# Gathering raw tokens with 1/rms in the one-hot rows, finishing the output projection by token tile, and bias casts on ScalarE, in a one-core hybrid decoder layer

## The chip, the cores and the metric

One NeuronCore of a Trainium2 chip runs the whole layer; the other seven stay idle. The core has five engines with a queue each, worked off in order: PE (TensorE, matrix products), DVE (VectorE), ACT (ScalarE), POOL (GpSimd) and SP (SyncE, which here only issues DMAs). The metric is the device time of one launch in microseconds (us): the median of three runs before is 1156.03 us (1154.72 to 1156.2).

## The reference, cut to what matters

256 tokens of width 1024 go through one layer: two attention branches, their merge and output projection, then an expert network and a gated embedding. The change touches the end of the output projection and the entrance to the experts:

```python
x = x + merged @ w_out                        # residual stream, 256 x 1024
h = rmsnorm(x, g_ffn)                         # x / rms(x) * g_ffn
logits = h @ w_router + b_router              # 32 experts
top_vals, top_idx = lax.top_k(logits, 4)
top_w = softmax(top_vals)                     # each token goes to 4 experts
gu = xb @ w_gate_up[e] + b_gate_up[e]         # xb: the rows of h that chose expert e
g, u = min(gu[:, :1024], 7), clip(gu[:, 1024:], -7, 7)
y = ((u + 1) * g * sigmoid(1.702 * g)) @ w_down[e] + b_down[e]
x = x + (sum over a token's experts of top_w * y)
```

All weights are float32; the 32 experts have 8.4 MB (gate and up) and 4.2 MB (down) each.

## The kernel before, in words

Tokens lie in two tiles (`tt` = 0, 1) of 128 partitions. The residual stream `xs` is a tile of 128 x 2 x 1024 float32. The stages run one after the other: projections, attention with the gate units beside it, the branch merge into `mT`, the output projection (L676 to L696), norm and routing (L700 to L742), and a loop over 32 experts (L991 on).

**The weight stream.** Ten SBUF slots of 2 MB hold what the experts need. `release` (L152) is called where a slot's last user has been written down; it gives the slot to the next 2 MB piece of a fixed sequence (`seq`) and issues its DMA on SP's queue, which then waits until the last user is done. The sequence starts with the four gate/up pieces of expert 0 and the four of expert 1, then the two down pieces of expert 0. Slots 0 and 1 hold operands of the output projection (`mT` in slot 0, split weights in slot 1) and are released at its end (`release(0, 1, 2)`); slot 2 holds split weights of earlier units and is free sooner; slot 3 holds `b96`, the raw gate/up bias, and is released after the bias casts. The eleventh piece of the stream can only be issued when expert 0 has used its first one.

**The output projection.** Its weights come in eight units, each split into a high and a low part (cast on ACT, difference on DVE, L216 and L220). For each half `dh` of the columns and each of four units, twelve matmuls run: six for tile 0, six for tile 1 (three products per piece, L260 to L262). Then DVE adds each tile to `xs` (L694) and ACT takes the sum of squares (L695).

**Routing.** `raw_T(tt, dh)` (L667) transposes half a tile of `xs` on PE (`hT`), copies it on ACT (L672) and multiplies it with the router weights (`lg`, L674). The halves `dh` = 0 of both tiles are done inside the last projection half, the halves `dh` = 1 after it. One `rsqrt` for both tiles (thirteen small DVE operations) gives 1/rms, with which ACT makes `h_perm`, a scaled and permuted copy of `xs` (L717). DVE then picks the top four per token, and PE computes each token's place in its expert's list (`pos`, L739 to L741). `keep_warm` puts idle matmuls into PE's queue, 30 ahead of `pos` and 8 behind it.

**Bias.** `b_gate_up` is held in bfloat16 as three terms: sixteen casts and eight subtractions of 512 columns (L703 to L709), all on DVE.

**Gather.** For each pair of experts DVE builds one-hot rows `oh` from the places, and PE multiplies `h_perm` by them (L814 to L822): 16 matmuls per tile pair and column half. `ow`, the same rows times the router weights (L834), later brings the results back.

A scheduler orders each engine's instructions from the program's order, its dependences and its own cost estimates, so the order that is run differs from that of the code.

Of the kernel before, what the change touches and what calls it, by code (L numbers as in the profile page):

```python
# [65 lines left out]
def hybrid_layer(ctx, tc, x, p, b_down, w_ple_gate, w_ple_proj, bgu3, xt, tabs, wpre, wgu, wdn, out):  # L66
# [15 lines left out]
    def tok(tt):  # L82
        return slice(tt * P, (tt + 1) * P)

    def rsqrt(pool, ss, n, dim, name):

        m = pool.tile([P, n], F32, tag=f"rs_m{n}", name=f"{name}_m")
        V.tensor_scalar(m, ss, 1.0 / dim, EPS, op0=ALU.mult, op1=ALU.add)
        sh = pool.tile([P, n], I32, tag=f"rs_s{n}", name=f"{name}_s")
        V.tensor_single_scalar(sh, m.bitcast(I32), 1, op=ALU.logical_shift_right)  # L90
        r = pool.tile([P, n], F32, tag=f"rs_r{name}", name=f"{name}_r")
        V.tensor_scalar(r.bitcast(I32), sh, -1.0, RSQRT_MAGIC, op0=ALU.mult, op1=ALU.add)
        t = pool.tile([P, n], F32, tag=f"rs_t{n}", name=f"{name}_t")
        for _ in range(3):
            V.tensor_tensor(t, r, r, op=ALU.mult)
            V.scalar_tensor_tensor(t, in0=t, scalar=-0.5, in1=m, op0=ALU.mult, op1=ALU.mult)
            V.scalar_tensor_tensor(r, in0=t, scalar=1.5, in1=r, op0=ALU.add, op1=ALU.mult)
        return r
# [576 lines left out]

    lgb = [bank("lg") for _ in range(2)]  # L676
    for dh in range(2):
        bs = [bank("wo") for _ in range(2)]
        for kk in range(4):
            wh, wl = unit(2)  # L680
            for tt in range(2):
                for j in range(2):
                    k = 2 * kk + j
                    three([(bs[tt], (mT[0][:, k, tok(tt)], mT[1][:, k, tok(tt)]), (wh[:, j], wl[:, j]))],
                          k == 0, k == 7)
            for after, i in ((1, 8), (3, 9)):
                if 4 * dh + kk == after:
                    release(i)
            if dh == 1 and kk == 1:
                raw_T(0, 0)  # L690
                raw_T(1, 0)
        for tt in range(2):
            xv = xs[:, tt, dh * 512:(dh + 1) * 512]
            V.scalar_tensor_tensor(xv, in0=bs[tt], scalar=0.5, in1=xv, op0=ALU.mult, op1=ALU.add)  # L694
            A.activation(bank("sq"), xv, AF.Square, accum_out=hss[:, dh, tt:tt + 1])  # L695
    release(0, 1, 2)  # L696

    for i in range(3):
        r = slice(i * NE, (i + 1) * NE)
        V.tensor_copy(id96[r], ident[r, r])  # L700
    for c in range(0, 2048, 512):
        c = slice(c, c + 512)
        V.tensor_copy(bgu[:, c], b96[:, c])  # L703
        V.tensor_tensor(b96[:, c], b96[:, c], bgu[:, c], op=ALU.subtract)
        V.tensor_copy(bgu[NE:2 * NE, c], b96[NE:2 * NE, c])
        r = slice(2 * NE, 3 * NE)
        V.tensor_copy(bgu[r, c], b96[r, c])
        V.tensor_tensor(b96[r, c], b96[r, c], bgu[r, c], op=ALU.subtract)
        V.tensor_copy(bgu[r, c], b96[r, c])  # L709
    release(3)  # L710
    h_perm = keep.tile([P, 2, D], F32, tag="h8", name="h_perm")
    for tt in range(2):
# [3 lines left out]
    for tt in range(2):  # L716
# [11 lines left out]
    ohe = keep.tile([P, 2, 4, NE], F32, name="ohe")  # L728
    for tt in range(2):
        V.scalar_tensor_tensor(lg[:, tt], in0=lgb[tt][:, :NE], scalar=hrs[:, tt:tt + 1], in1=brb,  # L730
                               op0=ALU.mult, op1=ALU.add)
# [62 lines left out]

    def gather(pm, base):

        oh = work("oh", [P, 2, CAP])
        for tt in range(2):
            V.tensor_scalar(oh[:, tt], iota[:, 0:CAP], float(base), pm(tt), op0=ALU.add, op1=ALU.is_equal)
        b = shared("g")  # L800
        for k in range(8):
            for tt in range(2):
                T.matmul(b[:, k * CAP:(k + 1) * CAP], h_perm[:, tt, k * P:(k + 1) * P], oh[:, tt],
                         start=(tt == 0), stop=(tt == 1))
# [3 lines left out]
        return xg, oh  # L808

    def gather_pair(e):  # L810

        oh = work("oh", [P, 2, 2 * CAP])
        for tt in range(2):
            V.tensor_tensor(oh[:, tt].rearrange("p (j c) -> p j c", j=2), iota.rearrange("p (j c) -> p j c", j=2),  # L814
                            posm[:, tt, e:e + 2].unsqueeze(2).broadcast_to([P, 2, CAP]), op=ALU.is_equal)
        xg = work("xg", [P, 8, 2 * CAP])
        for half in range(2):
            b = psum("gu"[half])
            ks = slice(half * 4, half * 4 + 4)
            for k in range(4):  # L820
# [5 lines left out]
        return xg, oh  # L826

    def weigh(ow, oh, wv_, odd):  # L830
        for tt in range(2):
            o = ow[:, tt].rearrange("p (g c) -> p g c", g=4)
            o = o[:, 1:3] if odd else o[:, 0:4:3]
            V.tensor_scalar(o, oh[:, tt:tt + 1].broadcast_to([P, 2, CAP]), wv_(tt), None, op0=ALU.mult)  # L834

    def weigh_pair(e, oh):
        ow = work("ow", [P, 2, S])
        for j in range(2):
            weigh(ow, oh[:, :, j * CAP:(j + 1) * CAP], wv_of(e + j), j)
        return ow  # L840
# [81 lines left out]
    def overflow(room):  # L922
# [18 lines left out]
        with tc.If(v > OVER):  # L941
            V.memset(ow, 0.0)
            with tc.For_i(0, NE, 1) as e:
# [42 lines left out]

    xg2, oh2 = gather_pair(0)
    weights()
    ow = weigh_pair(0, oh2)
    ht = None  # L990
    for e in range(NE):  # L991
# [166 lines left out]
```

## Time and profile before

| | |
|---|---|
| median of 3 runs | 1156.03 us |
| the profiled execution's own time | 1153.93 us |
| its span, first to last instruction | 1151.9 us |
| PE busy | 1077.9 us (94%) |
| DVE busy | 328.4 us (29%) |
| ACT busy | 209.5 us (18%) |
| POOL busy | 79.0 us (7%) |
| HBM read | 438.21 MB |

The 2.0 us between span and time lie outside the first and last instruction. Times in rows are counted from the span's start. In a timeline row the columns are start, duration, engine, line, operation, what is written and read, shape, and in brackets how long the engine had been idle and whom it waited for. [...]

### The profile page before, as it was taken

What the parts mean: (1) busy time and instruction counts of PE and PEld (TensorE: products, weight loads), DVE (VectorE), ACT (ScalarE), POOL (GpSimd) and SP (SyncE); (2) the same over time, 40 slices, a digit from 0 to 9 for tenths busy, and PEclk for the clock granted to TensorE, in tenths of its full rate; (3) what the DMA queues carried; (4) which work ended last, traced back from release to release, by engine and by line L of the source; (5) the groups of instructions that cost most, each with busy time, mean ns of one, the idle gap of its engine ahead of it and who ended that gap; (6) DMA issues with size and microseconds to landing.
All of it is one profiled execution on the core that took longest, in us unless ns stands there. A gap on an engine that the chain in (4) does not pass through costs nothing. (4 is left out here: it accounts for less than half of the span.)

```text
span 1151.9 us, 13101 instructions
## 1 busy us (share of the span) xinstructions
PE 1077.9 (94%) x5446; PEld 524.7 (46%) x5446; DVE 328.4 (29%) x730; ACT 209.5 (18%) x393; POOL 79.0 (7%) x82
## 2 busy tenths in 40 slices
PE   9799999999999999998889999998998989898988
PEld 7688997543434343342333434343433333333336
DVE  5679688321111121111110111120111111111136
ACT  5576753110000000000001000000000000000024
POOL 5752320000000000000000000000000000000000
PEclk9999999999999999999999999998999999999999
DMA  9544569999999999999999999999999999999991
GB/s 369 189 146 147 183 201 356 374 428 431 432 429 432 430 430 431 431 428 414 430 431 431 429 432 430 430 431 427 431 431 432 427 431 431 430 431 431 428 387 42
DMA packets 40079, 440.15 MB, mean 382 GB/s; under 512 B 4432, under 2 KB 5200, under 8 KB 14832
## 3 DMA queue, kind: packets, MB, share of 16 engines
q1 hardware_dynamic: 40016, 439.27, 91.3%
q8 instruction: 44, 0.72, 0.2%
q14 instruction: 19, 0.16, 0.0%
HBM read 438.21 MB, written 1.05 MB: 381 GB/s over the span
## 5 line engine op out<-in xcount | busy, mean ns | idle before, releaser
L861 PE MATMUL g<-w_g,xg 128*64 128x512 f32 x1024 | 294.5, 600 | 22.0 <-DMA w_g<-in_wgu 17.4
L861 PE MATMUL u<-w_g,xg 128*64 128x512 f32 x1024 | 290.9, 595 | 0.0
L885 PE MATMUL y<-w_d,ht 128*64 128x512 f32 x992 | 227.0, 597 | 11.9 <-DMA w_d<-in_wdn 11.9
L861 PEld LDWEIGHTS g<-w_g,xg 128*64 128x64 f32 x1024 | 78.7, 137 | 167.2 <-issue 122.6
L865 DVE TENSOR_SCALAR g<-g 128x512 f32<-128x512 f32 x32 | 22.1, 692 | 462.2 <-PE g L855 462.2
L861 PEld LDWEIGHTS u<-w_g,xg 128*64 128x64 f32 x1024 | 82.5, 138 | 146.7 <-issue 143.9
L885 PEld LDWEIGHTS y<-w_d,ht 128*64 128x64 f32 x992 | 69.1, 136 | 132.3 <-issue 114.7
L867 ACT ACTIVATE th<-g 128x512 f32<-128x512 f32 x32 | 20.2, 632 | 478.7 <-DVE g L865 478.7
L890 DVE COPY ys<-y 64x512 f32<-64x512 f32 x31 | 21.5, 694 | 168.7 <-ACT ys L889 168.7
L895 PE MATMUL acc<-ys,owT 128*128 128x512 f32 x128 | 59.4, 605 | 8.8 <-ACT ys L889 8.8
L889 ACT COPY ys<-y 64x512 f32<-64x512 f32 x31 | 18.0, 580 | 263.2 <-PE y L885 263.2
L895 PEld LDWEIGHTS acc<-ys,owT 128*128 128x128 f32 x128 | 22.9, 189 | 45.3 <-ACT ys L889 21.1
L822 PE MATMUL g<-oh,h_perm 128*128 128x128 f32 x256 | 33.3, 282 | 6.3 <-DVE g L865 6.2
L822 PEld LDWEIGHTS g<-oh,h_perm 128*128 128x128 f32 x256 | 29.9, 191 | 16.9 <-DVE g L865 11.7
L822 PEld LDWEIGHTS u<-oh,h_perm 128*128 128x128 f32 x256 | 29.8, 192 | 8.1 <-issue 8.1
L220 POOL TENSOR_TENSOR fr<-raw_x,fr 128x384 fp32r<-128x384 f32 (+1 forms) x21 | 29.2, 1399 | 47.8 <-ACT fr L216 47.8
L822 PE MATMUL u<-oh,h_perm 128*128 128x128 f32 x256 | 32.2, 279 | 0.0
L261 PE MATMUL proj<-fr,fr 128*128 128x512 f32 (+1 forms) x64 | 26.2, 409 | 5.6 <-DVE fr L220 5.4
L260 PE MATMUL gate<-fr,fr 128*128 128x256 f32 x104 | 30.5, 293 | 0.0
L262 PE MATMUL gate<-fr,fr 128*128 128x256 f32 x104 | 29.6, 285 | 0.7 <-DVE fr L220 0.7
L834 DVE TENSOR_SCALAR ow<-oh,whalf 128x128 f32<-128x128 f32 x64 | 14.0, 283 | 54.6 <-PE owT L847 54.6
L261 PE MATMUL gate<-fr,fr 128*128 128x256 f32 x104 | 29.4, 283 | 0.0
(320 smaller groups left out, 1161.2 us busy)
## 6 DMA issues: line engine op xcount, KB each, us to landing
w_g<-in_wgu SPq DMA_DIRECT2D x124, 2048.0 KB, 31.9
w_d<-in_wdn SPq DMA_DIRECT2D x62, 2048.0 KB, 32.6
raw_x<-in_wpre SPq DMA_DIRECT2D x29, 512.0 KB, 3.7
w_g<-in_wgu SPq DMA_DIRECT2D x8, 1024.0 KB, 27.9
raw<-in_wpre SPq DMA_DIRECT2D x12, 512.0 KB, 8.3
w_ple<-in_w_ple_gate SPq DMA_DIRECT2D x8, 512.0 KB, 10.0
raw_o<-in_wpre SPq DMA_DIRECT2D x4, 512.0 KB, 5.0
w_d<-in_wdn SPq DMA_DIRECT2D x2, 1024.0 KB, 25.8
```

The source lines that it names most:

```text
L220: o = e.tensor_tensor(lo[:, a:b], src[:, a:b], hi[:, a:b], op=ALU.subtract)
L260: T.matmul(o, lh, rh, start=first, stop=False)
L261: T.matmul(o, lh, rl, start=False, stop=False)
L262: T.matmul(o, ll, rh, start=False, stop=last)
L822: T.matmul(b[:, k * P:(k + 1) * P], h_perm[:, tt, (half * 4 + k) * P:(half * 4 + k + 1) * P], oh[:, tt], start=(tt == 0), stop=(tt == 1))
L861: T.matmul(gu[i][half * CAP:(half + 1) * CAP], xg[:, k], wv_, start=(k == 0), stop=False)
L865: V.tensor_scalar_min(g, gu[0], 7.0)
L867: A.activation(th, g, AF.Tanh, scale=0.851)
L885: T.matmul(y[g * CAP:(g + 1) * CAP], ht[:, f % 4, (f // 4) * CAP:(f // 4 + 1) * CAP], w[:, dh * 512:(dh + 1) * 512], start=(f == 0), stop= ...
L889: A.copy(ys[0:CAP, odd], y[0:CAP])
L890: V.tensor_copy(ys[CAP:P, 1 - odd], y[CAP:P])
L895: T.matmul(acc[tt][dh], owT[:, dh, tok(tt)], ys[:, dh], start=first, stop=last)
```

## The change

Three things are rewritten.

1. In the second half of the output projection, unit 6 isn't used when it comes; units 6 and 7 are used together, first all twelve matmuls of tile 0, then all twelve of tile 1. Residual, second transpose, 1/rms and routing are then written per tile, so that those of tile 0 stand ahead of tile 1's. `tc.issue_after` keeps tile 1's residual behind tile 0's `rsqrt`.
2. `h_perm` is dropped. The gather multiplies `xs` itself, read with a step of 8 elements (`xk`), and 1/rms goes into the one-hot rows (is_equal, then times `hrs`). Since `oh` then holds 1/rms, `ow` is built from the places directly.
3. The sixteen bias casts move from DVE to ACT; the eight subtractions stay on DVE. They are written behind the projection as before.

```diff
-    for tt in range(2):
-        raw_T(tt, 1)
-    V.tensor_tensor(hss[:, 0], hss[:, 0], hss[:, 1], op=ALU.add)
-    hrs = rsqrt(wk, hss[:, 0], 2, D, "f")
-    for tt in range(2):
-        A.activation(h_perm[:, tt].rearrange("p (k q) -> p k q", k=8),
-                     xs[:, tt].rearrange("p (q k) -> p k q", k=8), AF.Copy, scale=hrs[:, tt:tt + 1])
-    keep_warm(WARM2)
...
+    def residual(tt, dh, b):
+        xv = xs[:, tt, dh * 512:(dh + 1) * 512]
+        V.scalar_tensor_tensor(xv, in0=b, scalar=0.5, in1=xv, op0=ALU.mult, op1=ALU.add)
+        A.activation(bank("sq"), xv, AF.Square, accum_out=hss[:, tt, dh:dh + 1])
+
+    hrs = [None, None]
+    for dh in range(2):
+        bs = [bank("wo") for _ in range(2)]
+        late_units = []
+        for kk in range(4):
+            late_units.append((kk, *unit(2)))
+            for after, i in ((1, 8), (3, 9)):
+                if 4 * dh + kk == after:
+                    release(i)
+            if dh and kk == 2:
+                continue
+            for tt in range(2):
+                for k2, wh, wl in late_units:
+                    for j in range(2):
+                        k = 2 * k2 + j
+                        three([(bs[tt], (mT[0][:, k, tok(tt)], mT[1][:, k, tok(tt)]), (wh[:, j], wl[:, j]))],
+                              k == 0, k == 7)
+                if dh and kk == 3:
+                    with tc.issue_after(last_step[0]) if tt else ExitStack():
+                        residual(tt, 1, bs[tt])
+                    raw_T(tt, 1)
+                    V.tensor_tensor(hss[:, tt, 0:1], hss[:, tt, 0:1], hss[:, tt, 1:2], op=ALU.add)
+                    hrs[tt] = rsqrt(keep, hss[:, tt, 0:1], 1, D, f"f{tt}")
+                    route(tt)
+            late_units = []
+            if dh == 1 and kk == 1:
+                raw_T(0, 0)
+                raw_T(1, 0)
+        if not dh:
+            for tt in range(2):
+                residual(tt, 0, bs[tt])
+    release(0, 1, 2)
...
-        V.tensor_copy(bgu[:, c], b96[:, c])
+        A.copy(bgu[:, c], b96[:, c])
         V.tensor_tensor(b96[:, c], b96[:, c], bgu[:, c], op=ALU.subtract)
-        V.tensor_copy(bgu[NE:2 * NE, c], b96[NE:2 * NE, c])
+        A.copy(bgu[NE:2 * NE, c], b96[NE:2 * NE, c])
         r = slice(2 * NE, 3 * NE)
-        V.tensor_copy(bgu[r, c], b96[r, c])
+        A.copy(bgu[r, c], b96[r, c])
         V.tensor_tensor(b96[r, c], b96[r, c], bgu[r, c], op=ALU.subtract)
-        V.tensor_copy(bgu[r, c], b96[r, c])
+        A.copy(bgu[r, c], b96[r, c])
...
+    xk = [xs[:, tt].rearrange("p (q k) -> p k q", k=8) for tt in range(2)]
...
         for tt in range(2):
-            V.tensor_tensor(oh[:, tt].rearrange("p (j c) -> p j c", j=2), iota.rearrange("p (j c) -> p j c", j=2),
-                            posm[:, tt, e:e + 2].unsqueeze(2).broadcast_to([P, 2, CAP]), op=ALU.is_equal)
+            for j in range(2):
+                V.tensor_scalar(oh[:, tt, j * CAP:(j + 1) * CAP], iota[:, 0:CAP], posm[:, tt, e + j:e + j + 1], hrs[tt],
+                                op0=ALU.is_equal, op1=ALU.mult)
...
-                    T.matmul(b[:, k * P:(k + 1) * P], h_perm[:, tt, (half * 4 + k) * P:(half * 4 + k + 1) * P],
+                    T.matmul(b[:, k * P:(k + 1) * P], xk[tt][:, half * 4 + k],
                              oh[:, tt], start=(tt == 0), stop=(tt == 1))
```

**ACT's queue** at the end of the output projection, before: `fr_80<-raw_x` and `fr_80<-pre_64` are the casts of units 6 and 7, `sq,fss<-xs` the squares, `raw_x<-hT` the copies of the transposes.

```order
L216 CAST fr_80<-raw_x 128x1024
L216 CAST fr_80<-pre_64 128x1024
L695 ACTIVATE sq,fss<-xs 128x512 x2
L672 COPY raw_x<-hT 128x4x128 x2
L695 ACTIVATE sq,fss<-xs 128x512 x2
L672 COPY raw_x<-hT 128x4x128 x2
L717 ACTIVATE h_perm<-xs,f_r 128x1024 x2
```

The same place in ACT's queue now, where `bgu<-b_1928` are the bias casts:

```order
L742 CAST bgu<-b_1928 96x512 x4
L218 CAST fr_80<-raw_x 128x1024
L744 CAST bgu<-b_1928 32x512
...
L702 ACTIVATE sq,fss<-xs 128x512
L218 CAST fr_80<-pre_64 128x1024
L702 ACTIVATE sq,fss<-xs 128x512
L748 CAST bgu<-b_1928 32x512
...
L746 CAST bgu<-b_1928 32x512
L748 CAST bgu<-b_1928 32x512
L674 COPY raw_x<-hT 128x4x128 x2
L702 ACTIVATE sq,fss<-xs 128x512
```

All sixteen casts now stand ahead of the first copy `raw_x<-hT`: four, then three, then nine directly in front of it.

**PE's queue** at the end of the output projection, before (`wo` the projection, `hT` the transposes, `lg` the router logits):

```order
L261 MATMUL wo<-fr_80,fr_79 128x512
L262 MATMUL wo<-fr_80,fr_79 128x512
L671 MATMUL hT<-cst,xs 128x128 x8
L281 LDWEIGHTS warm
L281 MATMUL warm<-warm 128x256
...
L674 MATMUL lg<-cst,raw_x 128x32 x4
L281 LDWEIGHTS warm
L281 MATMUL warm<-warm 128x256
L674 MATMUL lg<-cst,raw_x 128x32 x4
```

And now, from eight projection matmuls before the end:

```order
L673 MATMUL hT<-cst,xs 128x128 x4
L263 MATMUL wo<-fr_80,fr_79 128x512
L264 MATMUL wo<-fr_80,fr_79 128x512
...
L263 MATMUL wo<-fr_80,fr_79 128x512
L676 MATMUL lg<-cst,raw_x 128x32 x4
L264 MATMUL wo<-fr_80,fr_79 128x512
...
L264 MATMUL wo<-fr_80,fr_79 128x512
L673 MATMUL hT<-cst,xs 128x128 x4
L283 LDWEIGHTS warm
L283 MATMUL warm<-warm 128x256
```

Tile 0's second transposes and logits have moved in front of the last eight and four projection matmuls. The first halves, earlier on, keep their places: four `wo`, then `lg` for tile 0, `hT` for tile 1, four `wo`, `lg` for tile 1. SP's queue has the same order in both.

## Rows read from the trace of the kernel before

**Rows 1.** Windows: busy us by engine, granted clock, DMA share, GB/s.

```profile
300.00:600.00 300.00, 284.74 (x1380) 111.65 (x1376) 49.94 (x96) 20.93 (x37) 0.00 (x0) 1.00 1.01 429
198.00:200.00 2.00, 1.58 (x11) 1.10 (x11) 0.86 (x3) 1.44 (x5) 0.00 (x0) 1.00 0.94 344
212.00:220.00 8.00, 8.00 (x39) 2.66 (x39) 1.09 (x3) 0.00 (x0) 0.00 (x0) 1.00 0.65 229
```

**Rows 2.** Timeline of SP's queue: weight pieces issued around the routing.

```profile
189.04 0.33 SPq L80 DMA_DIRECT2D w_d<-in_wdn  x1
197.29 0.80 SPq L80 DMA_DIRECT2D w_g<-in_wgu  x2
215.93 10.63 SPq L80 DMA_DIRECT2D w_g<-in_wgu  x4
```

**Rows 3.** Timeline of PE: end of the output projection.

```profile
190.22 1.06 PE L674 MATMUL lg<-cst,raw_x 128*128 128x32 f32 x8
194.13 0.39 PE L262 MATMUL wo<-fr,fr 128*128 128x512 f32 x1
196.87 0.39 PE L262 MATMUL wo<-fr,fr 128*128 128x512 f32 x1
```

**Rows 4.** Timeline of DVE and ACT: first bias cast, first copy, `h_perm`.

```profile
180.22 0.42 DVE L703 CAST bgu<-b 96x512 bf16<-96x512 f32 x1 [2.08 <-DMA b<-in_bgu]
189.56 0.59 ACT L672 COPY raw_x<-hT 128x512 f32<-128x512 f32 x1 [2.76 <-PE hT L671]
202.50 4.19 ACT L717 ACTIVATE h_perm<-xs,f_r 128x1024 f32<-128x1024 f32 x2 [1.65 <-DVE f_r L97]
```

**Rows 5.** Windows: the stretch between the first bias cast and the first copy.

```profile
180.22:189.56 9.34, 9.34 (x45) 7.75 (x44) 9.16 (x15) 3.45 (x6) 0.00 (x0) 1.00 1.01 428
```

**Rows 6.** Timeline of ACT: two casts back to back.

```profile
46.86 1.03 ACT L216 CAST fr<-raw_x 128x1024 fp32r<-128x1024 f32 x1
47.79 1.04 ACT L216 CAST fr<-raw 128x1024 fp32r<-128x1024 f32 x1
```

**Rows 7.** Groups by shape, ACT and DVE, 512 columns: count | busy, mean ns | idle.

```profile
L216 ACT CAST fr<-raw_x 128x512 fp32r<-128x512 f32 x1 | 0.6, 623 | 0.3 <-PE proj L262 0.3
...
L708 DVE TENSOR_TENSOR b<-b,bgu 32x512 f32<-32x512 f32 x4 | 2.7, 684 | 0.1
```

**Rows 8.** Timeline of PE: restarts after two long waits.

```profile
44.43 0.50 PE L261 MATMUL proj<-fr,fr 128*128 128x512 f32 x1 [2.78 <-DVE fr L220]
57.33 0.50 PE L261 MATMUL proj<-fr,fr 128*128 128x512 f32 x1 [2.66 <-DVE fr L220]
```

**Rows 9.** Windows: the clock behind the first of these restarts.

```profile
44.00:46.00 2.00, 1.57 (x5) 1.33 (x6) 1.25 (x7) 0.54 (x2) 0.00 (x0) 0.80 0.21 37
46.00:48.00 2.00, 2.00 (x6) 1.51 (x6) 0.08 (x1) 2.00 (x5) 0.04 (x1) 0.50 0.61 225
48.00:50.00 2.00, 2.00 (x15) 1.83 (x14) 1.88 (x2) 1.97 (x4) 2.00 (x2) 0.85 0.18 29
```

**Rows 10.** Timeline of DVE and PE: selection done, places begun.

```profile
204.14 0.66 DVE L737 TENSOR_REDUCE sel<-ohe 128x32 f32<-128x128 f32 x2
206.76 0.31 PE L739 MATMUL pos<-sel,cst 128*128 128x32 f32 x2
```

**Rows 11.** One tile's or line's loads: count, ns min/median/max, first and last start.

```profile
L822 PEld LDWEIGHTS g<-oh,h_perm x256: 186/192/192, 208.5 to 1042.3; 128*128 128x128 f32 x128
L671 PEld LDWEIGHTS hT<-cst,xs x16: 138/140/226, 188.6 to 199.1; 128*128 128x128 f32 x16
L1042 PEld LDWEIGHTS y<-cst,xs x4: 189/192/193, 1122.6 to 1122.9; 128*128 128x128 f32 x4
```

**Rows 12.** Timeline of PE: bias matmuls of two experts, two experts apart.

```profile
402.37 0.40 PE L855 MATMUL g<-bgu,id 96*64 96x512 bf16 x2
455.65 0.40 PE L855 MATMUL g<-bgu,id 96*64 96x512 bf16 x2
```

More of the change, by code (lines that the diff above doesn't have):

```diff
@@ L83, in tok @@
         return slice(tt * P, (tt + 1) * P)
+    last_step = [None]
     def rsqrt(pool, ss, n, dim, name):
@@ L96, in rsqrt @@
             V.scalar_tensor_tensor(t, in0=t, scalar=-0.5, in1=m, op0=ALU.mult, op1=ALU.mult)
-            V.scalar_tensor_tensor(r, in0=t, scalar=1.5, in1=r, op0=ALU.add, op1=ALU.mult)
+            last_step[0] = V.scalar_tensor_tensor(r, in0=t, scalar=1.5, in1=r, op0=ALU.add, op1=ALU.mult).ins
         return r
@@ L674, in raw_T @@
             T.matmul(lgb[tt][:, :NE], hrT[:, k, tok(tt)], w_r[:, k], start=(k == 0), stop=(k == 7))
[L676 to L680, printed above, removed]
-            for tt in range(2):
[L682 to L691, printed above, removed]
-        for tt in range(2):
[L693 to L702, printed above, removed]
-        V.tensor_copy(bgu[:, c], b96[:, c])
-        V.tensor_tensor(b96[:, c], b96[:, c], bgu[:, c], op=ALU.subtract)
-        V.tensor_copy(bgu[NE:2 * NE, c], b96[NE:2 * NE, c])
-        r = slice(2 * NE, 3 * NE)
-        V.tensor_copy(bgu[r, c], b96[r, c])
-        V.tensor_tensor(b96[r, c], b96[r, c], bgu[r, c], op=ALU.subtract)
-        V.tensor_copy(bgu[r, c], b96[r, c])
-    release(3)
-    h_perm = keep.tile([P, 2, D], F32, tag="h8", name="h_perm")
-    for tt in range(2):
-        raw_T(tt, 1)
-    V.tensor_tensor(hss[:, 0], hss[:, 0], hss[:, 1], op=ALU.add)
-    hrs = rsqrt(wk, hss[:, 0], 2, D, "f")
-    for tt in range(2):
-        A.activation(h_perm[:, tt].rearrange("p (k q) -> p k q", k=8),
-                     xs[:, tt].rearrange("p (q k) -> p k q", k=8), AF.Copy, scale=hrs[:, tt:tt + 1])
-    keep_warm(WARM2)
     sel = keep.tile([P, 2, NE], F32, name="sel")
@@ L728, in hybrid_layer, with route @@
     ohe = keep.tile([P, 2, 4, NE], F32, name="ohe")
-    for tt in range(2):
-        V.scalar_tensor_tensor(lg[:, tt], in0=lgb[tt][:, :NE], scalar=hrs[:, tt:tt + 1], in1=brb,
+    lgb = [bank("lg") for _ in range(2)]
+    def route(tt):
+        V.scalar_tensor_tensor(lg[:, tt], in0=lgb[tt][:, :NE], scalar=hrs[tt], in1=brb,
                                op0=ALU.mult, op1=ALU.add)
@@ L737, in hybrid_layer @@
         V.tensor_reduce(sel[:, tt], ohe[:, tt].rearrange("p j e -> p e j"), axis=AX.X, op=ALU.add)
+    def residual(tt, dh, b):
[34 more added lines that the diff above has]
+    release(0, 1, 2)
+    for i in range(3):
+        r = slice(i * NE, (i + 1) * NE)
+        V.tensor_copy(id96[r], ident[r, r])
+    for c in range(0, 2048, 512):
+        c = slice(c, c + 512)
+        A.copy(bgu[:, c], b96[:, c])
+        V.tensor_tensor(b96[:, c], b96[:, c], bgu[:, c], op=ALU.subtract)
+        A.copy(bgu[NE:2 * NE, c], b96[NE:2 * NE, c])
+        r = slice(2 * NE, 3 * NE)
+        A.copy(bgu[r, c], b96[r, c])
+        V.tensor_tensor(b96[r, c], b96[r, c], bgu[r, c], op=ALU.subtract)
+        A.copy(bgu[r, c], b96[r, c])
+    release(3)
+    keep_warm(WARM2)
     b = bank("pos")
@@ L793, in down_bias, with gather @@
                 T.matmul(acc[tt][dh], wT[:, tok(tt)], bdn[:, dh * 512:(dh + 1) * 512], start=False, stop=False)
-    def gather(pm, base):
+    xk = [xs[:, tt].rearrange("p (q k) -> p k q", k=8) for tt in range(2)]
+    def gather(pm):
         oh = work("oh", [P, 2, CAP])
         for tt in range(2):
-            V.tensor_scalar(oh[:, tt], iota[:, 0:CAP], float(base), pm(tt), op0=ALU.add, op1=ALU.is_equal)
+            V.tensor_scalar(oh[:, tt], iota[:, 0:CAP], pm(tt), hrs[tt], op0=ALU.is_equal, op1=ALU.mult)
         b = shared("g")
@@ L802, in gather @@
             for tt in range(2):
-                T.matmul(b[:, k * CAP:(k + 1) * CAP], h_perm[:, tt, k * P:(k + 1) * P], oh[:, tt],
+                T.matmul(b[:, k * CAP:(k + 1) * CAP], xk[tt][:, k], oh[:, tt],
                          start=(tt == 0), stop=(tt == 1))
@@ L825, in gather_pair, with weigh @@
                             gpk[:, 1, ks].unsqueeze(2).broadcast_to([P, 4, 2 * CAP]), op=ALU.mult)
-        return xg, oh
-    def weigh(ow, oh, wv_, odd):
+        return xg
+    def weigh(ow, pm, wv_, odd):
         for tt in range(2):
@@ L949, in overflow @@
                 for c in EXTRA_CHUNKS:
-                    xg, oh = gather(lambda tt: pmd[:, tt:tt + 1], c * CAP)
-                    weigh(ow, oh, lambda tt: wvd[:, tt:tt + 1], 0)
+                    V.tensor_scalar_add(pmd, pmd, float(-CAP))
+                    xg = gather(lambda tt: pmd[:, tt:tt + 1])
+                    weigh(ow, lambda tt: pmd[:, tt:tt + 1], lambda tt: wvd[:, tt:tt + 1], 0)
                     owT = combine_T(ow)
@@ L1005, in hybrid_layer @@
         if odd and not last:
-            xg2, oh2 = gather_pair(e + 1)
-            ow = weigh_pair(e + 1, oh2)
+            xg2 = gather_pair(e + 1)
+            ow = weigh_pair(e + 1)
         ht = hidden_T(u, "th" if last else "ht")
```

12 lines of the change are left out of this document (6 added, 6 removed).

## The prediction

> **What bounds the kernel now.** I read the windows first. From 300 to 600 us the DMA engines are busy all the time and move 429 GB/s [rows 1]. A 2 MB piece (2.10 MB) thus takes 4.9 us, and the 12.6 MB of one expert 29.3 us. PE, busy as it looks, does two experts in 53.3 us [rows 12], against 58.7 us for their weights; it starts the experts behind the stream, since ten slots are full by then, and catches up. So the end of the program is the end of the weight stream, and a microsecond in which the stream stands still while its slots are blocked is a microsecond of time. What PE, DVE or ACT do is worth something only where it moves such a standstill.
>
> The windows show where the stream stands still around the change: from 198 to 200 the rate is 344 GB/s, 0.4 us lost; from 212 to 220 it is 229 GB/s, (429 - 229) x 8 / 429 = 3.7 us lost [rows 1]. SP's queue says why [rows 2]. The first down piece is issued at 189.04. The next pieces wait for slots 0 and 1, which the last projection matmul frees (it starts at 196.87 and ends at 197.26 [rows 3]), and are issued at 197.29, just before the queue runs dry at about 198.5. With the piece behind them they last 3 x 4.9 = 14.7 us, to about 213.7 (a window that loses 0.4 lies between). The next issue is at 215.93, when expert 0 has used its first piece: 2.2 us too late, and 3.7 - 2.2 = 1.5 us more until the stream is back at full rate. Both places together cost 4.1 us, and that is the most this change can win.
>
> So two distances count: when the projection ends, and how long it is from there to expert 0's first release (215.93 - 197.26 = 18.7 us now).
>
> **Bias casts on ACT.** The bias arrives at 180.22 [rows 4]. From there to the first copy `raw_x<-hT` at 189.56, ACT is busy 3.45 us of 9.34 [rows 5]. All sixteen casts now stand ahead of that copy. ACT's cast of 512 columns takes 0.62 us [rows 7], and of back-to-back casts the second starts 0.1 us before the first one's end (47.79 against 46.86 + 1.03 [rows 6]), so 0.52 us each: 8.3 us. ACT then has 3.45 + 8.3 = 11.8 us of work from 180.22, to 192.0. The last of the four chunks is a chain of cast, subtraction on DVE (0.68 us [rows 7]) and cast, with nothing to fill it: 192.7. The copy ends 0.6 us later, at 193.3. PE has four projection matmuls and then, in its queue, the logits of this very copy; before, it began them at 190.22 [rows 3], now at 193.4. Everything behind them on PE waits, the rest of the projection first: **3.1 us**. Bounds, since no row shows an ACT cast to bfloat16: with DVE's 0.42 us [rows 4] for each and no wait in the last chain, the logits start at 191.3 (a stall of 1.1 us); with the full 0.62 us, no overlap and the wait, at 195.0 (4.8 us). I take the value of the ACT row. The time that DVE is relieved of (its casts) is worth nothing: it would have ended before 197.26 in any case.
>
> **Projection by token tile.** Tile 0's transposes and logits have moved ahead of the last eight and four projection matmuls. Their price on PE comes from what they take now: from 190.22 to 194.13 PE does two sets of logits, one of transposes and seven projection matmuls; twelve such matmuls take 196.87 - 194.13 = 2.74 us, seven 1.6 us, so 2.3 us remain, and one set of each costs about 1.35 us. The projection therefore ends at 197.26 + 3.1 + 1.35 = 201.7.
>
> **The clock.** A stall of 3.1 us is long for PE. After waits of 2.78 and 2.66 us [rows 8] PE restarts at full clock, and behind the first of them the granted clock is 0.80, 0.50 and 0.85 in the next six microseconds [rows 9]: (0.20 + 0.50 + 0.15) x 2 = 1.7 us lost. Here the stretch behind the stall is solid projection, so I add 1.7 us: the projection ends at **203.4**. Bounds: 0 and 1.7.
>
> **From there to the first release.** Before, the selection of both tiles is done at 204.80, but the places wait on PE to 206.76, behind idle matmuls [rows 10]: 2.0 us. `h_perm` (4.19 us from 202.50 [rows 4]) ends before that and costs nothing, so neither does dropping it win anything on this path. With tile 0's routing off the path (it runs beside tile 1's matmuls) I take away another 1.1 us, the second residual, square and copy; two more small DVE operations for the one-hot rows give 0.2 back. That is 18.7 - 2.0 - 1.1 + 0.2 = 15.8 us; bounds 14.5 (the idle matmuls never in the way) and 18.7 (all stays).
>
> **The sum.** With the projection's end at 203.4 the two pieces are issued 4.9 us after the queue ran dry at 198.5 (its piece of 189.04 hangs on unit 5, which the change leaves where it is); with the 1.5 us of a restart 6.4 us are lost. The three pieces then last to 203.4 + 1.5 + 14.7 = 219.6, and expert 0's first release comes at 203.4 + 15.8 = 219.2. An issue 1.2 us ahead of running dry lost 0.4 us, one at that point would lose 1.5, so 0.4 ahead costs about 1.1. Together 7.5 us instead of 4.1: **3.4 us slower**. The profiled execution took 1153.93 us (span 1151.9), so it would take 1157.3; that execution is 2.1 us below the median of 1156.03, so the median becomes **1159.4 us**.
>
> **The gather.** A pair's 16 gather matmuls now load `xs` with a step of 32 bytes. The trace has this step: transposes of such columns load in 192 ns against 140 ns for contiguous ones, while the gather's loads take 192 ns already [rows 11]. If they grew by the same 52 ns and all of it showed, the 32 loads in the trace would cost 1.7 us a pair. PE's spare time of 58.7 - 53.3 = 5.4 us a pair covers that in the loop; only the first gather, ahead of the first release, would pay it. I take 0 for the loop and for the first gather, and keep 1.7 as the other end. [...] The DVE operations per pair (four instead of two for `oh`) lie in PE's spare time too.
>
> **Rivals.**
> - *The clock holds.* Same stall, projection end at 201.7: 3.2 + 1.5 = 4.7 us, and the second place as above 1.1: 1.7 us slower, 1157.7. For it: the part behind the stall begins with logits and transposes, not with the same work as in rows 8. Against: both waits of that length were followed by the low clock.
> - *ACT's casts are no bottleneck* and the change does what its parts suggest. The copy isn't late; the projection ends at 197.26 + 1.35 = 198.6, the issue comes as the queue runs dry (1.5 us lost), the pieces last to 214.8, the release comes at 214.4 (1.1 us lost): 2.6 instead of 4.1, so 1.5 us faster, 1154.5. With the shortest distance, 14.5, the second loss is about 0.2: 2.4 us faster, 1153.6. It decides from the point where ACT's work ahead of the copy fits into the 5.9 us that were idle, 0.37 us a cast; no row of ACT with 512 columns is that short.
> - *The strided read shows.* 1.7 us more on the first gather: the release comes 1.3 us after running dry instead of before it, 2.8 us lost there instead of 1.1: 1161.1 with the stall and the low clock. For it: rows 11. Against: a load lies beside the matmul ahead of it.
>
> **Chances and range.** My forecast 0.46, the clock holds 0.25, ACT no bottleneck (or a stall near its lower bound) 0.20, strided read 0.09. Two kernels within 0.2%, 2.3 us, can't be told from no change here: below 1153.7 is faster, above 1158.3 slower. Slower takes 0.37 of my forecast (the rest of it, with a milder loss, is within), 0.03 of the second case and all of the last: 0.49. Faster needs the best form of the third case: 0.13. The same: 0.38. The range goes from 1153.7, at the better end of the third case, to 1161.8, above the last.
>
> **What would show it.** In the changed profile ACT's copy `raw_x<-hT` starts near 192.7 instead of 189.56; PE shows an idle time of about 3 us before `lg`, released by ACT; the clock falls to 0.50 for some microseconds behind it; the last `wo` matmul starts near 203; SP issues two gate pieces near 203.4 and the next near 219.2; the windows of DMA show a hole from 198.5 to about 204, and hardly one near 219. PE's period of two experts stays near 53.3 us until PE has caught up. If the copy starts before 190.5, or the hole at 198.5 is shorter than 2 us, the forecast is wrong in its main step; if all that is as said and the time isn't longer, then the stream isn't what sets the end.

## The result and the profile after

The changed kernel takes **1192.45 us** (median of 6 runs, 1190.31 to 1196.99); the kernel before took 1155.38 us in the runs beside it. The ratio is 1.0326, with a 95% interval of 1.0305 to 1.0347: 37 us slower, outside the range that was forecast. The profiled execution has a span of 1188.6 us.

The stretch of the routing, in windows (busy us of PE, PEld, DVE, ACT, POOL, then the granted clock as a share of the full one, DMA share, GB/s):

```profile
190.00:192.00 2.00, 0.00 (x0) 0.00 (x0) 0.50 (x1) 1.98 (x4) 0.00 (x0) 0.96 1.05 451
192.00:194.00 2.00, 0.00 (x0) 0.00 (x0) 0.68 (x1) 1.23 (x3) 0.00 (x0) 0.50 1.02 434
194.00:196.00 2.00, 1.91 (x9) 1.91 (x10) 0.00 (x0) 0.04 (x1) 0.00 (x0) 0.50 0.96 410
196.00:198.00 2.00, 2.00 (x9) 1.71 (x8) 0.00 (x0) 0.59 (x1) 0.00 (x0) 0.50 0.98 418
198.00:200.00 2.00, 2.00 (x13) 1.82 (x12) 0.00 (x0) 0.00 (x0) 0.00 (x0) 0.83 0.16 66
198.00:208.00 10.00, 9.21 (x60) 7.50 (x59) 5.71 (x30) 2.55 (x6) 0.00 (x0) 0.97 0.27 80
220.00:228.00 8.00, 8.00 (x39) 2.92 (x40) 1.58 (x5) 0.00 (x0) 0.00 (x0) 1.00 0.51 172
```

TensorE does nothing from 190 to 194, works at a granted clock of 0.50 to 198, and the stream stands nearly still from 198 to 208 (80 GB/s) and moves 172 GB/s from 220 to 228. Where [rows 1] lost 0.4 and 3.7 us, these two places lose (429 - 80) x 10 / 429 = 8.1 and (429 - 172) x 8 / 429 = 4.8 us. The timelines of ACT, PE and SP name the cause of the first (after the duration and the operation, the idle time ahead and who ended it):

```profile
188.54 0.62 ACT L744 CAST bgu<-b 32x512 bf16<-32x512 f32 x1
...
191.46 0.61 ACT L746 CAST bgu<-b 32x512 bf16<-32x512 f32 x1
192.82 0.61 ACT L748 CAST bgu<-b 32x512 bf16<-32x512 f32 x1 [0.75 <-DVE b L747]
193.46 0.59 ACT L674 COPY raw_x<-hT 128x512 f32<-128x512 f32 x1
...
194.09 1.92 PE L676 MATMUL lg<-cst,raw_x 128*128 128x32 f32 x8 [4.31 <-ACT raw_x L674]
...
204.34 0.39 PE L264 MATMUL wo<-fr,fr 128*128 128x512 f32 x1
```

```profile
204.75 0.80 SPq L80 DMA_DIRECT2D w_g<-in_wgu  x2
...
224.27 10.63 SPq L80 DMA_DIRECT2D w_g<-in_wgu  x4
```

ACT's last bias cast ends just before its copy, which starts at 193.46 instead of 189.56 [rows 4]; PE waits 4.31 us; the projection's last matmul starts at 204.34 instead of 196.87 [rows 3]; the pieces are issued 7.5 us later than in [rows 2], the next ones 8.3 us later.

These two delays alone do not make 37 us. The gather does. First its loads and matmuls (line 838, which answers to line 822 of before: count, ns minimum/median/maximum), then PE's period of two experts, which answers to [rows 12]:

```profile
L838 PEld LDWEIGHTS g<-oh,xs x256: 312/334/340, 212.7 to 1081.1; 128*128 128x128 f32 x128
L838 PE MATMUL g<-oh,xs x256: 401/402/505, 212.7 to 1081.3; 128*128 128x128 f32 x128
```

```profile
424.11 0.40 PE L871 MATMUL g<-bgu,id 96*64 96x512 bf16 x2
481.45 0.40 PE L871 MATMUL g<-bgu,id 96*64 96x512 bf16 x2
```

A load takes 334 ns instead of 192 [rows 11], and two experts 57.34 us instead of 53.28. What ends last has changed with it. PE's waits (us in total, times, longest) no longer name a weight DMA, and SP waits longer for PE's `u` and `y` matmuls, which free the slots (385.9 and 311.4 us in all, 259.7 and 150.4 before). The longest of PE's waits:

```profile
PE acc L911 <- ACT ys L905: 8.8, 13, 0.7
PE g L838 <- DVE g L881: 6.2, 11, 0.6
...
PE g L877 <- PEq L957: 4.4, 1, 4.4
PE lg L676 <- ACT raw_x L674: 4.3, 1, 4.3
```

The same view of the kernel before begins otherwise:

```profile
PE g L861 <- DMA w_g<-in_wgu: 17.4, 19, 1.4
PE y L885 <- DMA w_d<-in_wdn: 11.9, 17, 1.3
```

So before, PE had caught up with the stream and waited for it; after, it never comes to wait for it, and the end of the program is the end of PE's work. From 600 to 900 us the stream itself is held up by its slots: it moves 411 GB/s, against 430 in the kernel before.

### The profile page after: what moved, and what is told of

Read it like the earlier page. It is cut to its first block, busy times and chain, and to the rows that moved or that the text cites. A ratio compares the mean times of both kernels' runs of the same rounds, so it can differ in the third digit from the quotient of the medians.

```text
span 1188.6 us, 13148 instructions
## 1 busy us (share of the span) xinstructions
PE 1138.4 (96%) x5446; PEld 592.0 (50%) x5446; DVE 337.6 (28%) x759; ACT 214.4 (18%) x407; POOL 78.5 (7%) x82
## 5 line engine op out<-in xcount | busy, mean ns | idle before, releaser
L901 PE MATMUL y<-w_d,ht 128*64 128x512 f32 x992 | 230.6, 604 | 0.0
L877 PEld LDWEIGHTS g<-w_g,xg 128*64 128x64 f32 x1024 | 81.4, 137 | 143.6 <-issue 136.8
L838 PE MATMUL g<-oh,xs 128*128 128x128 f32 x256 | 66.2, 413 | 6.4 <-DVE g L881 6.2
L838 PEld LDWEIGHTS g<-oh,xs 128*128 128x128 f32 x256 | 62.4, 333 | 17.0 <-DVE g L881 11.7
L838 PEld LDWEIGHTS u<-oh,xs 128*128 128x128 f32 x256 | 62.8, 336 | 8.1 <-issue 8.1
L838 PE MATMUL u<-oh,xs 128*128 128x128 f32 x256 | 65.1, 407 | 0.0
L840 DVE TENSOR_TENSOR xg<-u,cst 128x512 f32<-128x512 f32 x16 | 11.1, 692 | 90.1 <-PE u L838 90.1
L850 DVE TENSOR_SCALAR ow<-cst,posm,whalf 128x128 f32<-128x128 f32 x64 | 17.9, 343 | 54.0 <-PE owT L863 53.9
L262 PE MATMUL gate<-fr,fr 128*128 128x256 f32 x104 | 30.7, 295 | 0.0
L264 PE MATMUL gate<-fr,fr 128*128 128x256 f32 x104 | 29.7, 286 | 0.7 <-DVE fr L222 0.7
```

The costliest lines, as they stand in the source:

```text
L262: T.matmul(o, lh, rh, start=first, stop=False)
L264: T.matmul(o, ll, rh, start=False, stop=last)
L838: T.matmul(b[:, k * P:(k + 1) * P], xk[tt][:, half * 4 + k], oh[:, tt], start=(tt == 0), stop=(tt == 1))
L877: T.matmul(gu[i][half * CAP:(half + 1) * CAP], xg[:, k], wv_, start=(k == 0), stop=False)
L901: T.matmul(y[g * CAP:(g + 1) * CAP], ht[:, f % 4, (f // 4) * CAP:(f // 4 + 1) * CAP], w[:, dh * 512:(dh + 1) * 512], start=(f == 0), stop= ...
```

## Experiments

The theory after the result (A): the step of 32 bytes makes the gather's loads slow enough that PE becomes the bound. The rivals: the added VectorE work (B), the stall and the holes in the stream (C). A fourth cause (D) came up on the way.

**1. A contiguous copy for the gather**, all else as after:

```
+    x_perm = keep.tile([P, 2, 8, P], F32, tag="h8", name="x_perm")
+    for tt in range(2):
+        A.copy(x_perm[:, tt], xs[:, tt].rearrange("p (q k) -> p k q", k=8))
...
-    xk = [xs[:, tt].rearrange("p (q k) -> p k q", k=8) for tt in range(2)]
+    xk = [x_perm[:, tt] for tt in range(2)]
```

> The kernel after with one thing more: ScalarE copies the residual stream once into a column-contiguous buffer (unscaled; 1/rms stays in the one-hot rows), and the gather reads its stationary columns there. Theory A (the 32-byte step of the gather's weight loads makes TensorE the bound): the loads fall from 334 to about 192 ns, a pair's gather from 7.9 to about 3.8 us, the period of two experts from 57.3 to about 53.3 us, the end is again the end of the weight stream, and what is left against the kernel before is the late projection: 1158 to 1161 us. Rival B (the added VectorE work, four one-hot operations of a pair and the longer ow): the load time changes, the total stays within 5 us of 1192. Rival C (the stall behind the casts and the holes in the stream cost the time): total stays above 1180.

Measured: 1166.26 us, ratio to before 1.010 (1.008 to 1.012). The gather in its groups (count | busy us, mean ns | idle) and PE's waits:

```profile
L841 PE MATMUL g<-oh,x_perm 128*128 128x128 f32 x256 | 33.5, 282 | 6.4 <-DVE g L884 6.2
L841 PEld LDWEIGHTS g<-oh,x_perm 128*128 128x128 f32 x256 | 30.0, 191 | 17.0 <-DVE g L884 11.7
```

```profile
PE g L880 <- DMA w_g<-in_wgu: 22.1, 19, 1.8
PE y L904 <- DMA w_d<-in_wdn: 13.5, 18, 1.2
```

The loads are back at 191 ns, PE waits for weights again, and 26 us are gone with no other edit. B and C are out as main causes. But theory A said 1158 to 1161: some 6 us remain that it doesn't explain.

**2. Bias casts back on VectorE**, strided gather kept (`A.copy(bgu...)` becomes `V.tensor_copy(bgu...)` four times).

> The kernel after with the sixteen bias casts back on VectorE; the strided gather stays. Theory A: TensorE is the bound from the first gather on, so all that the stall moved shows and no more: the first gather comes 4 to 6 us earlier, total 1186 to 1189 us. Rival C: the stall is the cause, total back to 1155 to 1160 us. Rival B: as theory A here.

Measured: 1186.66 us, 1.0267 (1.0248 to 1.0287), as theory A has it: 5.8 us from the earlier start, and still 31 us over before.

**3. Both undone.**

> The kernel after with both: contiguous unscaled copy for the gather and bias casts on VectorE; only the routing by token tile, the order of the last output-weight units and 1/rms in the one-hot rows are left of the change. Theory A: stream-bound, no ACT stall, 1152 to 1156 us, at or a little under the kernel before. Rival B: about 1185 us, since the VectorE work is still there. Rival C: 1155 us as theory A, which then tells nothing by itself.

Measured: 1162.20 us, 1.0064 (1.0044 to 1.0084). Against run 1 the casts are worth 4.1 us in a kernel whose end is the stream's. The total misses theory A by 6 us, as in run 1. The windows show what both share:

```profile
600.00:900.00 300.00, 282.50 (x1314) 111.65 (x1310) 51.12 (x103) 23.57 (x41) 0.00 (x0) 0.99 1.01 427
```

The kernel before has 430 there:

```profile
600.00:900.00 300.00, 283.73 (x1318) 111.16 (x1320) 49.38 (x96) 24.25 (x42) 0.00 (x0) 0.99 1.01 430
```

The DMA engines are as busy (1.01), and move 0.7% less. That was true of all kernels of the changed kind, wherever PE did not hold the stream up (run 1 has 428 GB/s from 240 to 340 us and 427 from 700 to 800, the kernel before 430 in both).

**4. The kernel before with the strided gather alone** (the new `gather`, `gather_pair` and `weigh`, no `h_perm`; casts, projection and routing as before).

> The kernel before with the gather of the kernel after alone (residual stream read with its 32-byte step, 1/rms in the one-hot rows, no scaled copy); casts, projection and routing as before. Theory A: the pair period is 57.3 us, TensorE never catches up with the stream, 1186 to 1190 us. Rival C: within 3 us of 1155. If theory A holds in this run and e1 falls back, the strided read alone carries nine tenths of the loss.

Measured: 1186.41 us, 1.0276 (1.0253 to 1.0298). With run 1 this closes the main question from both sides: the strided gather put in, with the VectorE work that belongs to it, costs 32 us of the 37 (its slots lie at another address too, which run 10 shows to be hidden there), and the strided read taken out alone, with that VectorE work left in, gives 26 back.

**5. Bias casts on ScalarE alone**, in the kernel before.

> The kernel before with the sixteen bias casts on ScalarE and nothing else changed. The stall alone, in a kernel whose end is the end of the stream: the copy raw_x<-hT moves from 189.6 to about 192.7, TensorE idles about 3 us before the logits, the projection ends near 202 instead of 197.3 and the two gate pieces are issued 4 to 5 us after the queue ran dry. Theory A (a standstill of the stream is paid in full): 1157 to 1160 us against 1154.3, the slots start at the same address as before, so the rate from 300 to 600 stays 429 GB/s. Rival: the stall is made good by the shorter rest on VectorE, no more than 1 us.

Measured: 1160.12 us, 1.0051 (1.0036 to 1.0067). PE and SP, in time order:

```profile
193.97 1.08 PE L674 MATMUL lg<-cst,raw_x 128*128 128x32 f32 x8 [3.67 <-ACT raw_x L672]
```

```profile
202.65 0.80 SPq L80 DMA_DIRECT2D w_g<-in_wgu  x2
219.93 7.19 SPq L80 DMA_DIRECT2D w_g<-in_wgu  x3
```

The logits wait 3.67 us, the pieces come 5.4 us late, and the time follows: 4.1 to 7.7 us by the interval. The stall is real and is paid in full where the stream is the bound.

**6. The slots moved by 32 bytes.** Five new small tiles (scratch of the reciprocal root, now kept apart for each token tile) lie ahead of the weight slots. In the program before, the first slot begins at byte 43776 of each partition, in the changed one at 43936; these addresses follow from the sizes of the program's tiles, and no trace shows them. This run changes nothing in before but that address:

```
     id96 = keep.tile([96, NE], BF16, name="id96")
+    pad = keep.tile([P, 8], F32, name="pad")
```

> The kernel before with one unused tile of 32 bytes per partition ahead of the weight slots: no instruction changes, but the slots begin at byte 43808 of each partition (32 past a multiple of 64) instead of 43776 (a multiple of 64). In the kernel after they begin at 43936, also 32 past one, since five small tiles are new. Theory D (the slots' start address sets the stream's rate: 430 GB/s before, 427 in all five kernels of the changed kind): 427 GB/s in the steady stretches, some 0.6% of 920 us of stream, so 1159 to 1161 us. Rival B (the added VectorE work slows the stream): 430 GB/s, 1154 to 1155 us.

Measured: 1161.41 us, 1.0065 (1.0052 to 1.0078), with the same instructions. The steady window, against 429 in [rows 1]:

```profile
300.00:600.00 300.00, 282.14 (x1364) 110.44 (x1362) 49.34 (x95) 20.89 (x37) 0.00 (x0) 1.00 1.01 425
```

Theory D holds: the rate falls without any added VectorE work.

**7. Both undone, slots at a multiple of 64** (43968).

> The kernel of the run with both undone (1162.2 us), and 32 bytes of padding ahead of the slots, which then begin at 43968, a multiple of 64. Theory D: the steady rate is back at 430 GB/s, 5 to 7 us come back, 1155 to 1157 us. Rival B (added VectorE work): 427 GB/s and 1162 us as without padding. Rival E (the step that counts is 256 bytes, as before's 43776 is a multiple of it and 43968 is not): also 427 GB/s and 1162 us; the moved kernel before would then be slow too.

Measured: 1163.12 us, 1.0080 (1.0067 to 1.0094), rate 425 GB/s. Theory D in the form "multiple of 64" fails; rival E (256 bytes) stands.

**8. Before, slots at a multiple of 128 only** (43904).

> The kernel before with 128 unused bytes ahead of the weight slots, which then begin at 43904: a multiple of 128 but not of 256. No instruction changes. If multiples of 256 count (43776 is one; the offsets of 32, 160 and 192 past one all gave 425 to 428 GB/s): 427 GB/s and 1160 to 1162 us. If multiples of 128 are enough: 430 GB/s and 1153 to 1155 us.

Measured: 1160.41 us, 1.0045 (1.0031 to 1.0059).

```profile
300.00:600.00 300.00, 282.69 (x1368) 110.74 (x1366) 49.32 (x95) 20.89 (x37) 0.00 (x0) 1.00 1.01 426
```

128 is not enough either. Starts of 32, 128, 160 and 192 bytes past a multiple of 256 were all slow (425 or 426 GB/s from 300 to 600 us). One at a multiple of 256 was not (429); but that is always the same one, 43776, so that any multiple of 256 will do isn't shown.

**9. Both undone, slots at 43776 again** (the scratch back in the pool it had before, the two results in spare columns of an existing tile).

> The kernel with both undone (contiguous unscaled copy, bias casts on VectorE), and the reciprocal root's scratch tiles placed so that the slots begin at 43776 as before; what is left of the change is the routing by token tile, the order of the last units and 1/rms in the one-hot rows, with all its added VectorE work. Theory D (address): 430 GB/s and 1154 to 1157 us, since its two standstills in the trace (198 to 202, 216 to 220) come to about 1.4 us more than before's. Rival B (the VectorE work slows the stream): 427 GB/s, 1162 us.

Measured: 1156.94 us, 1.0009 (0.9992 to 1.0027); no difference from before that can be measured.

```profile
300.00:600.00 300.00, 285.18 (x1382) 112.24 (x1382) 54.35 (x109) 20.90 (x37) 0.00 (x0) 1.00 1.01 429
```

The rate is back with all the added VectorE work in place, so B is out. Of the 6 us that runs 1 and 3 left open, 5.3 were the address (1162.20 against 1156.94).

**10. The kernel after, slots at 43776.**

> The kernel after, all of it, with the slots beginning at 43776 again. Theory A (TensorE is the bound there, the causes don't add up but the larger one hides the others): the rate up to 600 us rises from 427 to 430 GB/s and the total stays within 2 us of 1192. Rival (the costs add): 7 us come back, 1185 us.

Measured: 1193.21 us, 1.0326 (1.0301 to 1.0350). The stream is faster (431 GB/s from 240 to 340 us, 428 in the kernel after), and nothing comes back (1192.45 us in the kernel after, where PE is the bound). Two of the three costs add up: 32 us for the strided gather (run 4) and 5.8 for the casts (run 2) make the 37. The third, the address, is hidden by the gather.

**11. At which step the load gets slow** (a single execution). The gather reads k 0 and 1 with a step of 4 bytes (line 821), k 2 and 3 with 8 (line 823), k 4 and 5 with 16 (line 825), k 6 and 7 with 32 (line 827):

```
+        A.copy(x_mix[:, tt, 256:512].rearrange("p (q k) -> p k q", k=2), src[:, 2:4])
+        A.copy(x_mix[:, tt, 512:1024].rearrange("p (q k) -> p k q", k=4)[:, 0:2], src[:, 4:6])
```

> The kernel after with the gather's weight loads at four steps in one run, each on a line of its own: k 0 and 1 from a contiguous copy, k 2 and 3 from a copy with a step of 8 bytes, k 4 and 5 with 16 bytes, k 6 and 7 from the residual stream itself with 32 bytes. Known ends: 192 ns at 4 bytes and about 334 ns at 32 bytes. [...] Rival (cost grows with the span read): 8 bytes about 215, 16 bytes about 260, 32 bytes 334 ns. The gather of a pair then takes 5 to 6 us instead of 7.9, and the total lies between 1165 and 1185 us.

```profile
L825 PEld LDWEIGHTS u<-oh,x_mix 128*128 128x128 f32 x128 | 31.2, 326 | 8.1 <-issue 8.1
L827 PEld LDWEIGHTS u<-oh,xs 128*128 128x128 f32 x128 | 32.2, 337 | 0.0
...
L823 PEld LDWEIGHTS g<-oh,x_mix 128*128 128x128 f32 x128 | 16.5, 196 | 0.8 <-issue 0.8
L821 PEld LDWEIGHTS g<-oh,x_mix 128*128 128x128 f32 x128 | 15.7, 191 | 16.2 <-DVE g L899 11.7 <-issue 3.2 <-DVE u L905 0.8
```

191, 196, 326 and 337 ns: of the four steps 4 and 8 bytes lie within 5 ns of each other, 16 and 32 within 11, and 130 ns lie between 8 and 16. A cost that grows with the span read would have been near 215 and 260 ns at 8 and 16 bytes; it is out. Why the load gets slow there, no run shows. With half of the loads slow two experts take 55.3 us, 2 us more than before and not 4, and PE still catches up with the stream:

```profile
970.47 1.94 PE L919 MATMUL y<-w_d,ht 128*64 128x512 f32 x8 [0.46 <-DMA w_d<-in_wdn]
```

From there on it waits for weights again, and the total, 1167.12 us, is about that of run 1.

**12. Half the casts on each engine** (each chunk's first two on ScalarE, the others on VectorE; copy made by GpSimd; slots at 43776).

> Token-tile routing and 1/rms in the one-hot rows kept; contiguous unscaled copy made by GpSimd; of each chunk's four bias casts two on ScalarE and two on VectorE; slots at 43776. Theory: ScalarE has 3.45 + 8 x 0.52 = 7.6 us of work in the 9.3 us ahead of its copy at 189.6 and VectorE is free before the first token tile's residual at 194.9, so neither stalls TensorE; the projection ends near 198.7, the second standstill nearly goes: 1.5 us less than before, 1151 to 1154 us. Rival: one of the two engines still holds TensorE for 1 to 2 us, 1154 to 1157 us.

Measured: 1159.30 us, 1.0034 (1.0021 to 1.0047): slower than before, and slower than the rival's range too. The rival's mechanism is there; ACT's queue again stood behind a cast:

```profile
190.62 0.62 ACT L746 CAST bgu<-b 32x512 bf16<-32x512 f32 x1 [0.89 <-DVE b L745]
191.26 0.59 ACT L675 COPY raw_x<-hT 128x512 f32<-128x512 f32 x1
...
191.90 1.56 PE L677 MATMUL lg<-cst,raw_x 128*128 128x32 f32 x8 [1.72 <-ACT raw_x L675]
```

The amount of work fitted, the order did not: the cast waits for VectorE's subtraction, and the copy for the cast. PE waits a second time, 1.70 us at 203.76, for tile 1's residual. It stands on VectorE behind tile 0's `rsqrt`, and that behind GpSimd's copy (last section, last point). SP issues the pieces at 202.09 and 219.41, 4.8 and 3.5 us later than before.

**13 and 14. Only the casts that wait for nothing go to ScalarE**; the others to GpSimd and VectorE (13) or VectorE alone (14); the contiguous copy on ScalarE behind its last copy for the logits:

```
-        A.copy(bgu[NE:2 * NE, c], b96[NE:2 * NE, c])
+        G.tensor_copy(bgu[NE:2 * NE, c], b96[NE:2 * NE, c])
...
-        A.copy(bgu[r, c], b96[r, c])
+        V.tensor_copy(bgu[r, c], b96[r, c])
...
+        with tc.issue_after(last_copy[0]):
+            A.copy(x_perm[:, tt], xs[:, tt].rearrange("p (q k) -> p k q", k=8))
```

> Token-tile routing and 1/rms in the one-hot rows kept, slots at 43776, contiguous unscaled copy on ScalarE behind the second tile's last copy. Of the sixteen casts the four that wait for nothing but the bias go to ScalarE (done by 182.1), the four of the second rows to GpSimd, which is idle, the eight in the chain stay on VectorE. Theory (the half-and-half run failed because ScalarE's queue stood behind casts that wait for VectorE's subtractions): ScalarE's copy starts at 189.2 to 189.6, VectorE has its last cast done near 193.4, TensorE has no idle time over 0.5 us before the first residual, the gate pieces are issued near 199 and the next near 215.5: 1153 to 1155.5 us, 1 to 2 us under the run with both undone and aligned. Rival (by tile, the order itself costs as much as it gains): 1156 us or more with no stall in the trace.

> As the run on three engines, without GpSimd: four casts on ScalarE, twelve on VectorE. VectorE ends its casts near 195.1, about when the first tile's last matmul ends (194.9), so TensorE idles up to 1 us there: 0.5 to 1 us more than the run on three engines, 1154 to 1156 us. If this run is the faster one, GpSimd's casts hold up VectorE.

Measured: 1153.74 us on three engines, 0.9988 (0.9978 to 0.9999), and 1153.90 us on two, 0.9991 (0.9977 to 1.0005). Run 13 in time order, ACT, PE and SP:

```profile
189.77 0.59 ACT L677 COPY raw_x<-hT 128x512 f32<-128x512 f32 x1 [1.60 <-PE hT L676]
...
190.43 1.06 PE L679 MATMUL lg<-cst,raw_x 128*128 128x32 f32 x8
```

```profile
199.46 0.80 SPq L80 DMA_DIRECT2D w_g<-in_wgu  x2
...
214.99 10.63 SPq L80 DMA_DIRECT2D w_g<-in_wgu  x4
```

No queue holds PE for long any more (its waits for the two residuals are 0.33 and 0.79 us), though VectorE's last cast ends at 195.2 and not at 193.4; the pieces come 2.2 us later than before, the next ones 0.9 us earlier. Run 13 is faster than before by 0.1 to 2.5 us, barely clear of noise; run 14 can't be told from before, nor the two from each other, so whether GpSimd's share matters they don't show.

## Why the prediction was wrong

*What bounds the kernel.* Right for the kernel before, wrong for the one after. The step that failed is the last part, on the gather: "PE's spare time of 58.7 - 53.3 = 5.4 us a pair covers that in the loop". Two things were off in it.

The price first. The bound of 52 ns a load was read from transposes [rows 11]; the gather's load grew by 334 - 192 = 142 ns, 2.7 times that. The chain of waits shows a pair's gather as two pieces of 16 matmuls:

```profile
856.35 4.03 PE g L838 x16
860.38 3.84 PE u L838 x16
```

7.87 us a pair; the periods of two experts differ by 57.34 - 53.28 = 4.06 us. The "other end" of 1.7 us was no upper bound.

Then what the price is held against. Even 4.1 us is less than 5.4, so by that sentence it would still have cost nothing. But the spare time was not spare: it is what PE catches up with. In the kernel before PE first waits for weights here:

```profile
532.50 1.08 PE L861 MATMUL g<-w_g,xg 128*64 128x512 f32 x4 [0.41 <-DMA w_g<-in_wgu]
```

From the first gather at 208.5 [rows 11] that is 324 us, 6.1 periods of 53.3 us, each gaining 5.4 us: by this estimate PE began about 33 us behind the stream. With 58.7 - 57.3 = 1.4 us in each of the 15 periods from the first pair to the last it could win back 21 us of these 33. It wins back less, since a period holds other work too: the one from 598.15 to 668.82, in which PE multiplies for the gated embedding, takes 70.7 us. The bias matmuls of the first and of the last pair, before and after:

```profile
226.01 0.40 PE L855 MATMUL g<-bgu,id 96*64 96x512 bf16 x2
1068.69 0.40 PE L855 MATMUL g<-bgu,id 96*64 96x512 bf16 x2
```

```profile
234.36 0.40 PE L871 MATMUL g<-bgu,id 96*64 96x512 bf16 x2
1106.89 0.40 PE L871 MATMUL g<-bgu,id 96*64 96x512 bf16 x2
```

The 15 periods take 842.7 us before and 872.5 after, against 15 x 58.7 = 880 for the weights: PE gains 8 us in all. The 29.8 us by which they are longer, and the 8.4 us by which PE starts later, are the loss (36.7 us between the two spans; the tail is 1.5 us shorter). PE never comes to wait for the stream, and each further microsecond of its work is a microsecond of time. Run 11 shows where the limit lies: at 2 us more a pair PE still reaches the stream, so at the prediction's own upper price of 1.7 us its conclusion on the loop would have held. At 4.1 us it fails. The prediction said that PE "starts the experts behind the stream [...] and catches up", and never asked how long it may take to.

*Bias casts on ACT.* Right in mechanism, a little small: the copy started at 193.46 (192.7 forecast), PE waited 4.31 us, and 3.67 in run 5, where the casts move alone. Counted as the prediction counts, from 190.22, the logits start 3.9 us late (194.09) and in run 5 3.75, where the stall was put at 3.1. The last cast did wait for DVE's subtraction, 0.75 us, as forecast; the size was off in the cast itself, 0.61 us long and one every 0.58 us (five steps from 188.54 to 191.46) where 0.52 were taken. The lower bound, logits at 191.3, comes out at about 191.0 from its own terms; no forecast rests on it.

*The clock.* Right: 0.50 behind the stall. From 194 to 200 it cost (0.50 + 0.50 + 0.17) x 2 = 2.3 us, where 1.7 were forecast.

*Projection by token tile, and the distance to the first release.* The last projection matmul starts at 204.34 against "near 203", and the stall (0.8 us) and the clock (0.6) account for the difference, so the term of 1.35 us held; from the issue at 204.75 to the release at 224.27 it is 19.5 us, of which the slower first gather is 4.1: 15.4 against 15.8 forecast. The term "0 for the first gather" was the error here; the second hole, forecast at 1.1 us, became 4.8.

*The sum.* Without the strided gather the time would have been inside the range: run 1, less the address, which runs 3 and 9 put at 5.3 us, is about 1161 us, with 1159.4 forecast. Against the kernel before in the runs beside it (1154.34) that is 6.6 us, though, where 3.4 were forecast: the direction was right, the size about half. The address was not in the prediction at all; in the kernel after it is hidden, so it isn't what made the forecast wrong.

*The rivals.* "The clock holds" and "ACT no bottleneck" are refuted by the windows above. "The strided read shows", with 0.09 the least likely, named the right place and priced only the first gather, 1.7 us. Its argument against ("a load lies beside the matmul ahead of it") fails on the rows of line 838: the matmuls grow with the loads, from a median of 275 ns (line 822 of before; run 1 has a mean of 282) to 402. The row in its favour, 192 against 140 ns [rows 11], was the right warning, and gave the transposes' price.

## What to carry to other kernels

An engine with spare time in each round may be using it to catch up: divide the backlog it starts with by what it gains in a round, count the rounds that hold other work, and charge an added cost against what is left over at the end, not against one round. Price an access by a row of the same instruction kind; here a transpose's load grew by 52 ns [rows 11] and the gather's by 142. When work moves to another engine, ask which instruction its queue will then stand behind, not only whether the time fits; and after any edit that adds small persistent tiles, look at where the large DMA targets have come to lie (32 bytes cost 429 - 425 = 4 GB/s in run 6).

## What the runs showed of the hardware

- A float32 weight load of 128 columns takes 191, 196, 326 and 337 ns at steps of 4, 8, 16 and 32 bytes (run 11), and the matmul with it 288, 282, 405 and 402 (means of the same groups). These rows say nothing of a moving operand in single floats at such steps. For runs of four floats whose starts are 32 bytes apart as a moving operand they show no cost: line 877 reads `w_g` so, line 901 reads `w_d` contiguously, and a matmul takes 597 and 604 ns (means, kernel after).
- The start of the DMA's target moves the rate by about 0.7%: 429 to 431 GB/s with slots at byte 43776, the one multiple of 256 that was tried, wherever PE does not hold the stream up (windows 240:300, 300:600, 600:900, 900:1100); 425 to 428 with starts 32, 128, 160 or 192 bytes past one, and 5 to 7.5 us of this kernel. A step of 256 bytes fits these runs; what makes the rate depend on the address no run shows.
- A VectorE operation on one element a partition took 1.48 us instead of 0.16 while GpSimd copied (run 12). It ended when that copy did (200.79 against 200.77 us), and a cast of four columns beside GpSimd's second copy took 1.43 us, where it takes 0.17 in run 13:

```profile
198.66 2.11 POOL L754 COPY x_perm<-xs 128x1024 f32<-128x1024 f32 x1 [32.65 <-DVE xs L703]
...
199.31 1.48 DVE L727 TENSOR_TENSOR fss<-fss 128x1 f32<-128x1 f32 x1 [0.79 <-ACT sq L704]
```
